# A quadrant swap by DMA alone: queues fed in coupled turns instead of a deep free-running queue

## The chip, the cores and the metric

The kernel runs on one core of one Trainium2 chip. The metric is the device time of the whole launch in microseconds (us); smaller is better. Several runs of each kernel are compared by their median.

## The reference

```python
def setup_inputs():
    return {"x": np.random.randn(8192, 8192).astype(np.float32)}

def reference(x):
    return np.fft.ifftshift(x)
```

For an even number of rows and columns this moves the four quadrants: output row r, left half, is input row (r + 4096) mod 8192, right half; and output row r, right half, is the same input row's left half. Nothing is computed. A half row is 4096 float32, 16 KB, contiguous in memory; rows are 32 KB apart. There are 16384 half rows, 268.44 MB to be read and as much to be written.

## The kernel before, in words

The data never enters the core's own memory. Every transfer is a DMA (`dma_start`) that reads half rows of `x` and writes them as half rows of `out`, both in the chip's large memory (HBM). Two of the core's instruction sequencers issue the DMAs, each on a queue of its own: `nc.sync` (SP, the queue that the profile calls q1) and `nc.scalar` (ACT, q10). Sixteen DMA engines serve both queues.

The helper `copy` issues one DMA of 256 half rows, 16 for each of the 16 engines (`per = 16`, `rows = 256`). Its access pattern has three dimensions: 16 entries one row apart, then 16 entries 16 rows apart, then the 4096 numbers of a half row. So each of the 16 entries of the outermost dimension stands for the half rows of one engine, and neighbouring engines work on neighbouring rows:

```python
dims = [[C, ENGINES], [step * C, per], [1, hc]]
```

The loop takes 1024 rows at a time, in four groups of 256. SP copies the left halves of the groups in the order 0, 1, 2, 3; ACT copies the right halves in the order 2, 3, 0, 1, so that the two queues are 512 rows apart. That makes 32 DMAs for each queue, of 4 MB each.

The order is that of the program. The framework gives the DMAs eight semaphores in turn, four for each queue, and puts a wait ahead of a DMA whose semaphore is still in use: so each queue has up to four DMAs in flight, 64 half rows for each engine, and the next is issued when the oldest has landed. At the end SP waits for all of them.

Of the kernel before, what the change touches and what calls it, by code (L numbers as in the profile page):

```python
# [1 line left out]

# [4 lines left out]


ENGINES = 16


@with_exitstack
def kernel(
    ctx: ExitStack,
    tc: tile.TileContext,
    x: bass.AP,
    out: bass.AP,
):
    nc = tc.nc
    R, C = x.shape  # L20
    hr = R // 2
    hc = C // 2
    per = 16
    rows = ENGINES * per

    def copy(queue, row, h, step):

        dims = [[C, ENGINES], [step * C, per], [1, hc]]
        queue.dma_start(
            out=bass.AP(out.tensor, out.offset + row * C + h, dims),  # L30
            in_=bass.AP(x.tensor, x.offset + (row + hr) % R * C + hc - h, dims),
        )

    for first in range(0, R, 4 * rows):
        for n in range(4):
            copy(nc.sync, first + n * rows, 0, ENGINES)
            copy(nc.scalar, first + (n + 2) % 4 * rows, hc, ENGINES)


# [1 line left out]
_INS = ['x']  # L43
_OUTS = [((8192, 8192), 'float32')]


def kernel(**inputs):
    import numpy as _np
    import concourse.bacc as _bacc
    import concourse.tile as _tile  # L50
    from concourse import mybir as _mybir
    from concourse.bass_utils import run_bass_kernel_spmd as _run

    nc = _bacc.Bacc("TRN2", target_bir_lowering=False, num_devices=1)  # L54
    arrays, args = {}, []
    for name in _INS:
        a = _np.ascontiguousarray(inputs[name])
        if a.dtype.kind in "iu":
            a = a.astype(_np.int64)
        arrays[f"in_{name}_dram"] = a  # L60
        args.append(nc.dram_tensor(f"in_{name}_dram", a.shape, _mybir.dt.from_np(a.dtype), kind="ExternalInput").ap())
    for i, (shape, dtype) in enumerate(_OUTS):
        dt = _mybir.dt.from_np(_np.dtype(dtype))
        args.append(nc.dram_tensor(f"out_{i}_dram", shape, dt, kind="ExternalOutput").ap())
    with _tile.TileContext(nc) as tc:
        kernel(tc, *args)
    r = _run(nc, [arrays], core_ids=[0])
    got = tuple(r.results[0][f"out_{i}_dram"] for i in range(len(_OUTS)))
    return got[0]
```

## Time and profile before

| | |
|---|---|
| runs | 815.96, 812.23, 815.3 us; median 815.3 |
| span of the profiled execution | 812.4 us (its own time is not given apart from the span; the span lies beside the lowest of the runs) |
| DMAs | 32 from SP, 32 from ACT, 4096 KB each |
| time of one issue, median | SP 571 ns, ACT 578 ns |
| first issue, last landing | 0.73 us, 811.5 us after the span's start |
| issue to landing | shortest 25.6, median 101.0, longest 103.4 us |
| moved | 268.44 MB read and 268.44 MB written |

How to read it: a DMA is cut into packets, here one of 16 KB for each half row and one of 4 bytes for each engine that reports its completion. The rows "DMA" and "GB/s" of a view cut its window into 40 slices and give the busy share of the 16 DMA engines and the bytes that they moved in each; a row that begins with a queue's name gives its packets, its megabytes and the time of its packets as a share of 16 engines' time. "L29" is the line that issues the DMAs. "SPq" is the sequencer of SP, whose waits are listed with their total, number and longest.

### The profile page before, as it was taken

The numbers are of one execution on the slowest core, as the hardware profiler recorded it, in microseconds if no ns is written. First come the engines' busy times: TensorE is split into PE (matmuls) and PEld (weight loads), VectorE is DVE, ScalarE is ACT, GpSimd is POOL, SyncE is SP. The second block draws the span as 40 slices with busy tenths as digits, with TensorE's granted clock in tenths as the row PEclk, the third lists the DMA queues.
The fourth block names the chain that finished last, engine by engine and source line by source line (L and its number), as shares of the span: only waits on it lengthen the run. The fifth ranks groups of instructions, "written<-read, shape, count | busy, mean of one in ns | idle before, by whom it ended". The sixth has DMA issues, their size and how long they took to land. (4 is left out here: it accounts for less than half of the span.)

```text
span 812.4 us, 109 instructions
## 1 busy us (share of the span) xinstructions
POOL 0.2 (0%) x4
## 2 busy tenths in 40 slices
POOL 0000000000000000000000000000000000000000
DMA  9999999999999999999999999999999999999998
GB/s 307 331 331 336 335 331 331 335 325 337 334 332 336 331 333 332 334 339 332 332 334 331 329 331 334 332 328 333 330 334 335 334 328 333 332 331 330 338 331 280
DMA packets 17408, 268.44 MB, mean 330 GB/s; under 512 B 1024, under 2 KB 1024, under 8 KB 1024
## 3 DMA queue, kind: packets, MB, share of 16 engines
q1 hardware_dynamic: 8704, 134.22, 49.7%
q10 hardware_dynamic: 8704, 134.22, 49.5%
HBM read 268.44 MB, written 268.44 MB: 661 GB/s over the span
## 5 line engine op out<-in xcount | busy, mean ns | idle before, releaser
L54 POOL MEMSET const-bfloat16-1.0<- 128x1 bf16 x1 | 0.1, 101 | 0.0
L54 POOL MEMSET const-uint8-127<- 128x1 uint8 x1 | 0.1, 101 | 0.0
L54 POOL MEMSET const-float32-0.0<- 128x1 f32 x1 | 0.1, 98 | 0.2 <-issue 0.2
L54 POOL MEMSET const-float32-1.0<- 128x1 f32 x1 | 0.1, 98 | 0.0
## 6 DMA issues: line engine op xcount, KB each, us to landing
out_dram<-in_x_dram SPq DMA_DIRECT2D x32, 4096.0 KB, 101.0
out_dram<-in_x_dram ACTq DMA_DIRECT2D x32, 4096.0 KB, 101.0
```

The lines of the kernel that those rows point to most:

```text
L54: nc = _bacc.Bacc("TRN2", target_bir_lowering=False, num_devices=1)
```

## The change

The transfers stay DMAs of half rows on the same two queues; their sizes, their access pattern and the moment at which they are issued change.

- The access pattern has two dimensions: 16 x per rows, one row apart, and the 4096 numbers of a half row. How the rows are divided among the 16 engines is no longer written out.
- The rows are taken in eight eighths of 1024 rows, each with its own entry (turn, rest) of `plan`. A turn gives each engine `turn` half rows on each queue (8 or 16). It is issued as two DMAs for each queue: a main part of `turn - rest` half rows per engine, and an end part of `rest`.
- Before a turn is issued, both sequencers wait until the main parts of all turns before it have landed, those of both queues. At that moment `rest` half rows per engine are left on each queue. `main0`, `main1`, `end0` and `end1` are the semaphores that count this, by 16 for each DMA.
- In the fifth eighth, `rest` is 0: its turns are issued without a wait and undivided.
- ACT works 512 rows away from SP within the same eighth, as before.
- The whole stands in a critical section, in which the framework places no waits of its own. SP waits for all semaphores at the end.

The DMAs of one queue become: eighths one to four, 16 DMAs each (8 turns; main parts of 4, 3, 2 and 1 half rows per engine, end parts of 4, 5, 6 and 7); eighth five, 8 DMAs of 8 half rows per engine; eighths six to eight, 8 DMAs each (4 turns; main parts of 12, 10 and 8, end parts of 4, 6 and 8). That is 96 for each queue, 192 in all.

```diff
-    per = 16
-    rows = ENGINES * per
-
-    def copy(queue, row, h, step):
+    def copy(queue, row, h, per, sem):
 
-        dims = [[C, ENGINES], [step * C, per], [1, hc]]
+        dims = [[C, ENGINES * per], [1, hc]]
+        dst = out.offset + row * C + h
+        src = x.offset + (row + hr) % R * C + hc - h
         queue.dma_start(
-            out=bass.AP(out.tensor, out.offset + row * C + h, dims),
-            in_=bass.AP(x.tensor, x.offset + (row + hr) % R * C + hc - h, dims),
-        )
+            out=bass.AP(out.tensor, dst, dims),
+            in_=bass.AP(x.tensor, src, dims),
+        ).then_inc(sem, ENGINES)
 
-    for first in range(0, R, 4 * rows):
-        for n in range(4):
-            copy(nc.sync, first + n * rows, 0, ENGINES)
-            copy(nc.scalar, first + (n + 2) % 4 * rows, hc, ENGINES)
+    part = 1024
+    plan = ((8, 4), (8, 5), (8, 6), (8, 7), (8, 0), (16, 4), (16, 6), (16, 8))
+
+    with tc.tile_critical(), ExitStack() as sems:
+        mains = [sems.enter_context(nc.semaphore(f"main{i}")) for i in range(2)]
+        ends = [sems.enter_context(nc.semaphore(f"end{i}")) for i in range(2)]
+        queues = (nc.sync, nc.scalar)
+        main = end = 0
+        for k, (turn, rest) in enumerate(plan):
+            rows = ENGINES * turn
+            for first in range(k * part, (k + 1) * part, rows):
+                other = k * part + (first - k * part + part // 2) % part
+                if rest:
+                    for queue in queues:
+                        for sem in mains:
+                            queue.wait_ge(sem, main)
+                for queue, row, h, m, e in zip(
+                    queues, (first, other), (0, hc), mains, ends
+                ):
+                    copy(queue, row, h, turn - rest, m)
+                    if rest:
+                        copy(queue, row + ENGINES * (turn - rest), h, rest, e)
+                main += ENGINES
+                end += ENGINES if rest else 0
+        for sem in mains:
+            nc.sync.wait_ge(sem, main)
+        for sem in ends:
+            nc.sync.wait_ge(sem, end)
```

## The prediction, made before the changed kernel ran

> **What bounds the kernel now.** I read the page first, then the DMA view in short windows at the start and the end, then the queue's own waits and the landings of the output tensor, then the packet and landing records themselves. The page:
>
> ```profile
> DMA  9999999999999999999999999999999999999998
> ...
> DMA packets 17408, 268.44 MB, mean 330 GB/s; under 512 B 1024, under 2 KB 1024, under 8 KB 1024
> ...
> q1 hardware_dynamic: 8704, 134.22, 49.7%
> q10 hardware_dynamic: 8704, 134.22, 49.5%
> ```
>
> No compute engine works. The 16 DMA engines are busy 49.7 + 49.5 = 99.2% of 812.4 us, 805.9 us. Of the 17408 packets, 1024 are the small completion writes (64 DMAs x 16 engines) and 16384 are half rows of 16 KB, 1024 for each engine. So a half row holds its engine for 805.9 / 1024 = 0.787 us, and 1% of that is 8.1 us of kernel. The packet records add two things: there are always 14 to 17 packets in flight, one for each engine, each starting within about 10 ns of the end of the one before; and a third of them take the shortest time, 0.611 us, the others up to 1.4. The kernel is therefore the packet time multiplied by 1024, plus two ends. Nothing that only changes when a packet is queued can shorten it, unless it changes how long a packet takes.
>
> Does the packet time move during the run? Stretches of the span (length, POOL busy, clock, DMA share, GB/s):
>
> ```profile
> 2.20:5.00 2.80, 0.00 (x0) 1.00 1.00 351
> 5.00:10.00 5.00, 0.00 (x0) 1.00 1.02 360
> 10.00:15.00 5.00, 0.00 (x0) 1.00 0.99 311
> ...
> 100.00:400.00 300.00, 0.00 (x0) 1.00 1.00 333
> 400.00:800.00 400.00, 0.00 (x0) 1.00 1.00 332
> ```
>
> It is fast for the first 8 us and flat afterwards. Between 2.1 and 5.0 us only q1 (SP's queue) has data, and 64 packets go by, four for each engine in 2.9 us, 0.725 each. The second and third packet of each engine average 0.62 and 0.67 us.
>
> The waits of SP's queue, and the last 12 us:
>
> ```profile
> SPq L29 <- DMA out_dram<-in_x_dram: 689.4, 28, 25.3
> SPq L65 <- DMA out_dram<-in_x_dram: 102.2, 2, 79.5
> ```
> ```profile
> 806.00:808.00 2.00, 0.00 (x0) 1.00 0.96 328
> 808.00:810.00 2.00, 0.00 (x0) 1.00 0.54 180
> 810.00:812.40 2.40, 0.00 (x0) 1.00 0.02 7
> ```
>
> The sequencers already wait on landings, 28 times, but with four DMAs of 16 half rows in flight on each queue, so each engine has some 100 us of work ahead (median to landing 101.0 us). None of those waits reaches an engine. In the landing records the 16 engines finish one DMA within 1.1 to 2.8 us of each other all through the run, so they do not drift apart; the ACT queue stays some 3.5 packets per engine behind SP's, the head start of the first 2.9 us.
>
> **The change part by part.**
>
> *Bytes and half rows.* The same 16384 half rows of 16 KB, on the same two queues, with the same left and right halves 512 rows apart. Cost 0.
>
> *More DMAs.* 64 become 192: in four eighths 8 turns x 2 queues x 2, in the fifth 8 x 2, in the last three 4 x 2 x 2. Issuing takes 0.571 us each (SP) or 0.578 (ACT); 96 for each sequencer is 55 us of 812, beside the transfers. Completion writes go from 64 to 192 per engine; one takes 9 ns in the records and the next half row starts 6 ns later, so 128 x 15 ns = **1.9 us**, on the path, since engines have no gaps. Bounds: 0 and, if every gap of the run was due to them, (808 - 805) / 64 x 128, about 5 us.
>
> *The waits at a turn.* There are 44 turns that wait, 32 of 8 half rows and 12 of 16. Before it issues, each sequencer waits until the main part of the turn before has landed from both queues; behind the wait stands only that sequencer's next issue. An engine then has `rest` half rows left on each queue, 2 x rest x 0.787 us of work: 6.3, 7.9, 9.4, 11.0 and 12.6 us for rest 4 to 8. What must fit under it: from the packet's end to its landing 0.39 us (24.34 to 24.73 in the records), from issue to first packet 2.16 - 0.73 = 1.43 us, the lead of the fastest engine, up to 2.8 us, and SP's lead over ACT, one packet here, as a main part of 64 rows should delay ACT's first packet by 64/256 of the 2.9 us seen at the start. For rest 4 this is 0.4 + 1.4 + 2.8 + 0.8 = 5.4 against 6.3 us. It fits narrowly at 4 and well from 5 on. The cover is the rest part; without it a turn would cost over 2 us. For the 16-row turns with rest 4, SP's main part is 192 rows, ACT may fall 2.2 us behind, and a fast engine could go dry for a moment. I take **0.5 us** over the 12 turns of rest 4; bounds 0 and 12 x 2 = 24 us.
>
> *One drain.* The fifth eighth has rest 0: its main semaphores count whole turns. The first turn of the sixth eighth therefore waits until everything has landed, and the engines stand idle. This costs the mean wait for the slowest engine, 2.1 us by the last stretches above (0.46 of 2.0 us, and 0.98 of 1.2 us up to the last packet at 811.2), or 1.2 us by the mean over landings; then 0.39 us to land, 0.1 for the wait, 1.43 to the first packet, and 0.2 as first packets take 1.05 us. Sum 3.3 to 4.2; I take **4.0 us**. It is the only stall written into the program.
>
> *Ends.* A critical section adds a handshake of the two sequencers ahead of the first issue and another after the last wait. Such handshakes are 0.4 to 0.7 us in the waits of before, and may overlap with what is there: **0.6 us** together, bounds 0 and 1.5.
>
> *Which rows an engine works on.* Before, the outermost dimension has 16 entries one row apart, so the engines work on neighbouring rows, 32 KB apart. Now one dimension of 16 x per rows is split over the engines. If each gets a run of rows, they stand per x 32 KB apart, 32 to 384 KB, different in each eighth; if they get every sixteenth, nothing changes. The trace has no addresses and only the one spacing. From below, the cost is bounded by the start's pace, 1024 x (0.725 - 0.787) = -63 us; from above by a slow stretch of the trace, 311 against 333 GB/s, +57 us. Both come from stretches under 10 us, and every long stretch gives 332 or 333, so I take the long rows: 0. The Trainium skill speaks against the change here: "DMA: Bandwidth & Descriptors", section "Latency and other measured facts", has copies between HBM tensors at 207 GB/s with a row pitch of 512 KiB, 164 at 2 MiB and 214 at full rate. By that ratio, as an estimate, the whole run at a 512 KiB spacing would be 812.4 x 214/207 = 840 us. No run here shows it yet.
>
> Sum: 1.9 + 0.5 + 4.0 + 0.6 + 0 = 7.0 us. On the profile's span 812.4 that is 819.4. The runs shown have a median of 815.3, 2.9 above the span, so I forecast **822**.
>
> **The rivals.**
>
> *Aligned engines copy faster.* Short turns could keep engines and queues in the ordered state of the start, in which a half row takes 0.725 us or less. If one packet in three keeps that, 341 x 0.062 = 21 us are won: 815.3 + 7 - 21 = 801. For it: the second and third packets at 0.62 to 0.67. Against: the pace is gone by 10 us although the engines are then still within 1.6 us of each other, and 1.4 or 2.5 us of spread go with the same 333 and 332 GB/s. A turn that finds its queues filled lines up nothing. It decides the sign once one packet in nine keeps the pace (7.0 / 0.062 = 113 packets). Chance 0.24.
>
> *The new spacing collides.* If engines further apart meet more often in memory, the share of packets at 0.611 us falls. It is 0.32 now, so the others average (0.787 - 0.32 x 0.611) / 0.68 = 0.870; at a share of 0.25 the mean is 0.805, +18 us: 840. For it: two thirds of the packets are already stretched. Against: nothing in the trace shows that spacing matters. The rule of the skill above would be this case, and its steps are larger pitches than any here. Chance 0.17.
>
> *Rest 4 is too short.* Each of the 12 turns of rest 4 runs dry by 1 us: 815.3 + 7 + 12 = 834. Chance 0.07.
>
> *Nothing is felt.* The drain lies in ACT's tail, the small writes are free: 815. Chance 0.12.
>
> **How the numbers follow.** Forecast 0.40. About 0.5% is what a measurement of this kernel can tell from no change, here 811.2 to 819.4. Faster: the first rival without its weakest outcomes, 0.22, and 0.02 of the forecast. Same: the last rival 0.12, 0.06 of the forecast, 0.02 of the first. Slower: 0.32 + 0.17 + 0.07. The range 800 to 840 holds the forecast, the drain and starved cases, and half of each of the two rivals about packet time (0.40 + 0.12 + 0.07 + 0.12 + 0.09 = 0.80). The forecast's own range is 817 to 828, from the bounds of its small terms.
>
> **What would show it.** By eighths of the span: a DMA share of 1.00 everywhere but one dip of about 4 us near 510 us; 3072 small packets; GB/s of 331 to 333 in every eighth. The layout rival shows as GB/s that differ between eighths with a full DMA share, lowest where engines are furthest apart (eighths five to eight). Starvation shows as a share under 1.00 in the first and sixth eighth alone. The first rival shows as GB/s above 340 in the first four eighths. I am wrong if the packet time changes by over 1%, since every other term is small.

## The result, and the profile after

The changed kernel takes 815.93 us (median of 18 runs, 814.11 to 818.22), the kernel before 812.39 us (18 runs beside it, 809.84 to 816.83). The ratio is 1.0037, with a 95% interval of 1.002 to 1.0053: slower by 3.0 us by the ratio and 3.5 by the medians, within the 0.5% that the prediction called no change, and half of the 0.8% that it forecast.

The page of the changed kernel (busy tenths and GB/s in 40 slices of 20 us, packets, queues):

```profile
DMA  8999999999999999999999998999999999999998
GB/s 295 334 332 334 335 334 334 329 339 336 330 333 338 334 337 334 330 337 332 329 330 340 333 336 281 336 330 331 335 333 334 330 330 333 336 333 336 327 333 283
DMA packets 19458, 268.46 MB, mean 330 GB/s; under 512 B 3072, under 2 KB 3072, under 8 KB 3072
...
q10 hardware_dynamic: 9728, 134.22, 49.9%
q1 hardware_dynamic: 9728, 134.22, 48.8%
```

Between the two ends all slices look like those of before but one, the 25th, at 281 GB/s. Stretches around it:

```profile
502.00:504.00 2.00, 0.00 (x0) 1.00 0.96 328
504.00:506.00 2.00, 0.00 (x0) 1.00 0.45 172
506.00:508.00 2.00, 0.00 (x0) 1.00 0.00 0
508.00:510.00 2.00, 0.00 (x0) 1.00 0.84 295
510.00:512.00 2.00, 0.00 (x0) 1.00 1.14 418
```

That is the drain. In the records the last half row ends at 506.5 us, the turn is released at 507.1 and the first new packet starts 1.3 us later, 1.9 us after that last end. The last 16 half rows had ended 1.1 us before the very last on average, and the first 16 new ones start 0.2 us after the first on average. Adding up, moment by moment, what is missing from 16 half rows in flight, the fifth eighth has 3.8 us of idle time and the other eighths without an end 0.6 to 1.3, about as much as in the kernel before (0.5 to 0.8): the drain holds the engines for 2.8 to 3.2 us, by which of the two is taken off. The short excess at 418 GB/s behind it resembles the fast start that the prediction saw at the beginning of the run; it lasts 2 us.

Stretches within the eighths, first to fourth and sixth to eighth:

```profile
2.40:100.00 97.60, 0.00 (x0) 1.00 1.00 334
102.00:200.00 98.00, 0.00 (x0) 1.00 1.00 334
203.00:300.00 97.00, 0.00 (x0) 1.00 1.00 334
304.00:400.00 96.00, 0.00 (x0) 1.00 1.00 334
...
510.00:600.00 90.00, 0.00 (x0) 1.00 0.99 333
610.00:700.00 90.00, 0.00 (x0) 1.00 1.00 333
710.00:806.00 96.00, 0.00 (x0) 1.00 1.00 333
```

Turns of 8 or 16, with 4 to 8 left, all move 333 or 334 GB/s with engines fully busy: neither starvation nor an effect of the spacing. SP's queue waits:

```profile
SPq L55 <- DMA out_dram<-in_x_dram: 710.1, 43, 115.7
```

There are 43 waits in place of 28, and apart from the one at the drain no stretch shows one that reaches an engine.

What remains is the packet time. The mean in the records is 0.7829 us, against 0.7865 before, 3.7 us over 1024 packets, and that gain was in nobody's sum. The experiments are about the drain, this gain, the completion writes, and the bounds that the prediction left wide.

Two sorts of numbers must be kept apart. The time of a run is 1.8 us over its span. By that, the profiled execution of before took 814.2 us and lies 1.8 us above the median of 18, while the one of the changed kernel (815.5) lies at its median. So profiles show 1.4 us between the kernels, and medians 3.5.

Of the experiments, the first four ran beside a kernel before of 813.5 us; the next four with an interval beside one of 822.6 and the last four beside one of 822.0, each group on a chip of its own. The kernel before is about 1.1% slower in the later two groups, and so is the mean packet: 0.781 to 0.785 us in the profiles of the first group, 0.791 to 0.796 in those of the others. Times are therefore compared within such a group, and ratios across them. The second profile of before and the two sweeps by eighths are single executions on a fourth chip.

### The profile page after: what moved, and what is told of

It reads as the page before. It is cut to its first block, busy times and chain, and to the rows that moved or that the text cites. A ratio compares the mean times of both kernels' runs of the same rounds, so it can differ in the third digit from the quotient of the medians.

```text
span 813.8 us, 332 instructions
## 1 busy us (share of the span) xinstructions
POOL 0.2 (0%) x4
```

## The experiments

**Layout alone, and layout put back.** The kernel before with the new pattern, and the changed kernel with the old one:

```diff
-        dims = [[C, ENGINES], [step * C, per], [1, hc]]
+        dims = [[C, ENGINES * per], [1, hc]]
```


> The kernel before with nothing but the two-dimensional access pattern (256 rows one row apart) in the 64 free-running DMAs. Profile of the changed kernel: a half row takes 0.7829 us against 0.7865, which is 1024 x 0.0036 = 3.7 us won and hides half of the costs. Theory L (the division of rows among engines makes the packets shorter): mean packet 0.783, ratio to before 0.9955. Theory Q (the two queues in step, a lead of 0.25 packets per engine in place of 2.5) and theory D (few half rows queued, turns): 0.7865, ratio 1.000. Theory N (the two profiles differ by chance, runs of one kernel spread by 0.8%): 1.000, mean packet anywhere in 0.782 to 0.790.


```diff
-        dims = [[C, ENGINES * per], [1, hc]]
+        dims = [[C, ENGINES], [ENGINES * C, per], [1, hc]]
```


> The changed kernel with the access pattern of before (16 entries one row apart, then steps of 16 rows) and all its turns and waits. Theory L: packets go back to 0.7865, 3.7 us slower than the changed kernel, ratio to before 1.008. Theories Q, D, N: same as the changed kernel, ratio 1.0037, within 1.002 to 1.0053.

Layout alone: 813.09 us, ratio 1.0002 (0.9985 to 1.0018), mean packet 0.7847. Layout put back: 814.93 us, 1.002 (1.0002 to 1.0038), mean packet 0.7833, and the dip is there again, near 507 us, with 4.5 us of idle time in that eighth. Theory L falls: the new pattern does not make the kernel faster, and the old one does not make the changed kernel slower.

**The drain moved to the end of the plan, and turns further ahead.**

```diff
-    plan = ((8, 4), (8, 5), (8, 6), (8, 7), (8, 0), (16, 4), (16, 6), (16, 8))
+    plan = ((8, 4), (8, 5), (8, 6), (8, 7), (16, 4), (16, 6), (16, 8), (8, 0))
```


> The changed kernel with the entry without waits moved from the fifth to the last place of the plan, so that no turn waits for everything to land. All theories: the dip near 506 us is gone, and with it the 3.2 us that the engines stood idle in that eighth beyond the others: ratio to before 1.0037 - 0.0039 = 0.9998. If the drain is paid back elsewhere (engines start again in order and run faster for a while) the gain is under 2 us: ratio over 1.0013.

For the second kernel, each turn takes one of four pairs of main semaphores and waits for its last use, four turns ago:

```diff
...
+                mains = lanes[lane]
-                if rest:
+                if rest and used[lane]:
                     for queue in queues:
                         for sem in mains:
-                            queue.wait_ge(sem, main)
+                            queue.wait_ge(sem, used[lane])
...
```


> As the kernel with the drain moved to the end, but a turn waits for the main parts of the fourth turn before it, not of the last, so that three more turns (24 or 48 half rows per engine and queue) stay queued; the number of DMAs and completion writes is the same. Theory D (few half rows queued make packets shorter): packets at 0.7865, 3.7 us slower than the kernel with the drain at the end, ratio about 1.004. Theories L, Q and N: the same as that kernel, ratio about 1.000, as the lead of the queues is set at the start by the small first DMAs in both.

Drain at the end: 812.18 us, 0.9986 (0.9967 to 1.0006), 2.75 us under the kernel with the old pattern, which has the drain and ran beside it. Where the dip was:

```profile
502.00:504.00 2.00, 0.00 (x0) 1.00 0.92 311
504.00:506.00 2.00, 0.00 (x0) 1.00 1.07 393
506.00:508.00 2.00, 0.00 (x0) 1.00 0.99 344
508.00:510.00 2.00, 0.00 (x0) 1.00 1.02 328
```

The engines are busy throughout. The deep turns gave 814.16 us, 1.0005 (0.9985 to 1.0025). That is 2 us more than the short turns, in the direction of theory D, which had 3.7; but the lead between the queues was 3.0 packets here and 0.9 there, so that theory Q would say the same, and the intervals overlap. (The lead is counted here as the half rows that one queue has started more than the other, per engine, as a mean over the run. By this count the kernel before has 3.3 and the changed kernel 0.9; the expectations have smaller figures for both, which this count does not give.) Its profile even has the shortest mean packet of the four, 0.7808, in a run of 809.8 us.

**The lead alone, own waits, larger turns, twice the DMAs.**

The kernel before, with the first DMA of each queue in four:

```diff
...
+            if first == 0 and n == 0:
+                for i in range(4):
+                    copy(nc.sync, i * 64, 0, ENGINES, 4)
+                    copy(nc.scalar, 2 * rows + i * 64, hc, ENGINES, 4)
+                continue
```


> The kernel before, free-running, with the first DMA of each queue cut into four of 4 half rows per engine, and nothing else. It was made to take the lead of one queue over the other away (2.5 packets per engine in the kernel before, 0.25 to 0.6 in the kernels with short turns, 2.5 in the kernel with deep turns). The traces so far show the second queue's first packet 2.8 to 2.9 us after the first queue's, with first DMAs of 64 and of 256 rows alike, so the cut may leave the lead where it is; the trace tells. Theory Q (queues in step make packets shorter): if the lead falls under 1, ratio 0.9975 (2 us won); if it stays, 1.000. Theory D (few half rows queued): 1.000 in either case.

The kernel with the drain at the end, each sequencer waiting for its own queue:

```diff
-                    for queue in queues:
-                        for sem in mains:
-                            queue.wait_ge(sem, main)
+                    for queue, sem in zip(queues, mains):
+                        queue.wait_ge(sem, main)
```


> The kernel with the drain at the end (812.2 us, 0.9986 of before), but each sequencer waits for its own queue's main part alone, so that the queues are kept short and not in step: one queue may lead by 2 to 3 packets all along. Theory Q: the 2 us against the kernel with deep turns are lost, ratio 1.001. Theory D: kept, ratio 0.9986. Theory N (the 2 us between the short and the deep turns were chance): anything from 0.998 to 1.001, and the kernels of this call scatter likewise.

One plan throughout, with 128 DMAs:

```diff
-    plan = ((8, 4), (8, 5), (8, 6), (8, 7), (8, 0), (16, 4), (16, 6), (16, 8))
+    plan = ((16, 6),) * 8
```


> Turns of 16 half rows, 6 left, in all eight eighths: 128 DMAs in place of 192, no drain, no eighth without waits. Theory D and Q: the packets as short as in the kernel with the drain at the end, and 64 fewer completion writes per engine x 15 ns = 1.0 us less: 811.2 us, ratio 0.9975, the fastest version. Theory N: 1.000 less nothing, 0.999 to 1.001.

In the kernel with the drain at the end, every DMA of over one half row per engine in two, on the same semaphore (`one` issues a single DMA, as `copy` did):

```diff
+        if per > 1:
+            one(queue, row, h, per // 2, sem)
+            one(queue, row + ENGINES * (per // 2), h, per - per // 2, sem)
+            return 2 * ENGINES
...
```


> The kernel with the drain at the end, every DMA of more than one half row per engine cut into two: 368 DMAs in place of 192, 176 more completion writes for each engine. If one costs 15 ns, as the prediction took it, 2.6 us more: 814.8 us, ratio 1.0018. If the writes are free, 812.2 and 0.9986. If a DMA has a larger cost of its own on the engines (0.1 us or more each), over 830 us.

| | us | ratio (interval) | lead, packets | queued |
|---|---|---|---|---|
| lead, first DMAs cut | 823.30 | 0.9995 (0.9974 to 1.0016) | 3.3 | deep |
| own waits | 823.32 | 1.0004 (0.9987 to 1.0021) | 3.1 | short |
| turns of 16, 6 left | 821.98 | 0.9993 (0.9976 to 1.001) | 1.5 | short |
| twice the DMAs | 822.62 | 0.9998 (0.9982 to 1.0014) | 0.7 | short |

The cut did not take the lead away: the second queue's first packet is again 3.0 us behind. So it says nothing on theory Q. The others do not part Q from D either; every interval holds 1.000. No version is measurably faster than the kernel before, and the 2 us of the earlier pair have not come back.

**The kernel before, profiled once more.** No edit.

> The kernel before once more, for a second profile. If the mean packet of 0.7865 us in its first profile was typical, it comes back within 0.0005. If the packet time itself is what varies from run to run (runs spread by 7 us, 0.9%), it follows the span: 1 us of span for each 1.0 ns of mean packet.

Span 809.0 us, mean packet 0.7826. Between two executions of the same kernel the packet time moved by 3.9 ns and the span by 3.4 us: as much as the gain that was to be explained. The packet time therefore moves with the execution or the chip, which these two profiles do not part, and a single profile does not give it to better than half a per cent. This fits theory N; that nothing else shortened the packets is not shown.

**Four drains and none.** The same 128 DMAs in two orders, in place of the plan of the changed kernel:

```diff
+    plan = ((8, 0), (16, 8)) * 4
```


> The turns of the changed kernel with the plan (8, 0), (16, 8) four times over: four turns wait until everything has landed, in place of one; 128 DMAs. If a drain costs what the engines stood idle in the changed kernel (3.2 us): 4 x 3.2 = 12.7 us more than the same turns without drains, a ratio between the two of 1.016. If most of it is given back by faster packets behind it: under 1.008. If the cause of the changed kernel's 0.37% is not the drain: no difference beyond 0.2%.


```diff
+    plan = ((16, 8),) * 4 + ((8, 0),) * 4
```


> The same turns in another order, (16, 8) four times and then (8, 0) four times: the same 128 DMAs of the same sizes, and no turn that waits for everything. Ratio to before 0.998 to 1.001, as the other kernels without a drain; no dip in the DMA share.

With four drains 835.5 us (5 runs), 1.0166 (1.014 to 1.0192); without, 822.87 us (12 runs), 1.0016 (0.9999 to 1.0034). The difference is 12.6 us, 3.2 us for each drain; by the two intervals it is uncertain by some 2.6 us. The two profiles differ by 12.6 us as well: 11.0 us of that is idle time of the engines, 2.8 us for each drain, and 1.6 us is packet time (0.7956 against 0.7940 us). The page of the kernel with four drains:

```profile
DMA  8999999999999999999999998999999999899998
GB/s 294 334 328 325 326 295 326 320 332 336 318 329 328 323 314 305 326 328 324 329 330 324 330 329 294 321 327 329 321 332 328 332 328 333 280 334 325 329 326 284
```

Dips of the GB/s stand at the 6th, the 15th and 16th, the 25th and the 35th slice, one behind each eighth without waits; a slice is 20.8 us here, so that 294 of 328 is 2.2 us of work missing, and the second dip is split over two slices.

**Completion writes on one chip.** The kernel with the drain at the end, and its twin with twice the DMAs, side by side:

> The kernel with the drain at the end of the plan once more (192 DMAs), for its twin with twice the DMAs on the same chip: ratio to before 0.9986 if the first result holds, 0.998 to 1.001 if all kernels without a drain are alike.

> The kernel with every DMA cut in two once more (368 DMAs): 176 more completion writes per engine than the kernel with the drain at the end. At 15 ns each 2.6 us more than that kernel (0.32%); at 3 ns, as the first comparison with 128 DMAs suggests, 0.5 us (0.06%).

821.97 us, 0.9999 (0.9981 to 1.0017), against 822.67 us, 1.0011 (0.9994 to 1.0028). The 176 more writes of each engine cost 0.7 us, 4 ns each, and that with an uncertainty larger than itself; 2.6 us would stand at its edge. By this pair the 128 writes that the change adds cost about 0.5 us, where the prediction had 1.9, but the pair alone does not exclude 1.9. The kernel before bounds them better: against it, the kernel with twice the DMAs has 304 more writes per engine, which at 15 ns are 4.6 us or 0.55%. It came out at 0.9998 and 1.0011, with intervals that end at 1.0014 and 1.0028. So 15 ns each does not fit, unless the turns win something back elsewhere; the higher of the two ends allows about 8 ns each, 1.0 us for 128 writes.

**How little may be left.**

```diff
-    plan = ((8, 4), (8, 5), (8, 6), (8, 7), (8, 0), (16, 4), (16, 6), (16, 8))
+    plan = ((8, 7), (8, 5), (8, 4), (8, 3), (8, 2), (8, 1), (16, 2), (16, 1))
```


> The changed kernel with the plan 8 turns each of rest 7, 5, 4, 3, 2, 1 (turns of 8) and 4 turns each of rest 2, 1 (turns of 16). It looks for the rest at which engines run dry. By the prediction's sum (0.4 to land, 1.4 from issue to packet, up to 2.8 of spread, against 1.57 us for each half row left on both queues): idle time under 0.3 us per turn for rest 4 and more; at rest 3 (4.7 us of cover) the fastest engines run dry, 0.1 to 0.5 us per turn; at rest 2 (3.1) 0.5 to 1.5; at rest 1 (1.6) 1.5 to 2.5. Against it: no idle time at rest 3 and 2, if the spread of the engines counts for less than the prediction took.

Its eighths in order, ends left out:

```profile
5.00:100.00 95.00, 0.00 (x0) 1.00 1.00 334
105.00:200.00 95.00, 0.00 (x0) 1.00 1.00 333
206.00:300.00 94.00, 0.00 (x0) 1.00 1.00 334
307.00:405.00 98.00, 0.00 (x0) 1.00 0.98 328
410.00:514.00 104.00, 0.00 (x0) 1.00 0.92 311
519.00:625.00 106.00, 0.00 (x0) 1.00 0.89 302
632.00:730.00 98.00, 0.00 (x0) 1.00 0.96 324
737.00:838.00 101.00, 0.00 (x0) 1.00 0.94 315
```

With 7, 5 and 4 left the engines stay busy. At 3 the eighth has 3.6 us of idle time, against 0.6 to 0.8 in those three: 0.35 us per turn. At 2 it is 1.2 us per turn, at 1 it is 1.6, and with turns of 16 the same (1.1 and 1.6). So the cover that a turn needs lies between 4.7 us (3 left) and 6.3 us (4 left).

**How far apart engines may work.** The kernel before, with the rows of neighbouring engines 1, 16, 32 and 64 rows apart, twice over; over 1, the 16 half rows of an engine in one DMA follow one another:

```diff
-        dims = [[C, ENGINES], [step * C, per], [1, hc]]
+        dims = [[space * C, ENGINES], [step * C, per], [1, hc]]
...
```


> The kernel before, free-running, with the engines' rows 1, 16, 32, 64, 1, 16, 32, 64 rows apart in the eight eighths (32 KB, 512 KB, 1 MB, 2 MB); within an engine the rows follow one another where the spacing is over 1. The layout rival of the prediction: GB/s lower at 512 KB by 3% (a packet of 0.81 us), and by over 20% at 2 MB. No effect of spacing: 331 to 334 GB/s in each eighth.

Its eighths (32 KB, 512 KB, 1 MB, 2 MB, and again):

```profile
10.00:100.00 90.00, 0.00 (x0) 1.00 1.00 333
110.00:200.00 90.00, 0.00 (x0) 1.00 0.99 333
212.00:325.00 113.00, 0.00 (x0) 1.00 1.00 269
337.00:465.00 128.00, 0.00 (x0) 1.00 0.99 235
480.00:570.00 90.00, 0.00 (x0) 1.00 1.00 333
580.00:670.00 90.00, 0.00 (x0) 1.00 1.00 334
682.00:795.00 113.00, 0.00 (x0) 1.00 1.00 265
808.00:940.00 132.00, 0.00 (x0) 1.00 1.00 238
```

Up to 512 KB the spacing is free. At 1 MB the mean packet is 0.98 us, at 2 MB 1.10, and the DMA share stays at 0.99 to 1.00: busy is not the same as fast. In the 2 MB eighths the two queues work 32 rows apart, in the others 512 rows, so the loss at 2 MB is not shown to be due to the engines' spacing alone; the step from 512 KB to 1 MB has no such second difference.

## Why the prediction was right or wrong

*What bounds the kernel* held: packets one behind the other, 1024 for each engine, in every kernel here.

*The drain* held in mechanism and nearly in size: 4.0 us forecast, 2.8 to 3.2 measured in idle time and 3.2 by the runs with four. Its mis-sized part is the wait for the slowest engine. The prediction took 2.1 us from the end of the run; ahead of the drain it was 1.1 us. The way from the last end to the first new packet was forecast at 0.39 + 0.1 + 1.43 = 1.9 us and took 1.9. The drain is the one term that the runs show clearly: the two kernels with the change's single drain are at 1.0037 and 1.002, the kernels in turns without one between 0.9986 and 1.0016, and the one with four at 1.0166.

*The sum* is the step that failed: its terms were mis-sized, 7.0 us in all against 3.5 by the medians. Beside the drain there were 1.9 for completion writes, 0.5 for rest 4 and 0.6 for the ends. The ends held: the first packet is 0.2 us later, and the span goes on 0.4 us longer after the last landing. Rest 4 shows no idle time that stands out (0.6 us in its eighth where the rest was varied). The largest miss is the writes: about 0.5, at most about 1.0 by the bound above. What failed for them is the count of small gaps: 9 ns of a record and 6 ns to the next packet were summed as if the 16 engines lost them. (The upper bound beside that term, about 5 us, is 6 by its own figures.) Engines that share a memory may get a little of such a gap back; that is argued, not shown. In place of 7.0 stands 3.2 + 0.5 + 0.6 = 4.3 us; the medians differ by 3.5 and the interval reaches from 1.6 to 4.3. The kernels without a drain come out at 1.000 within 0.2%, so the smaller terms are below what these runs can tell.

*The level* was off by nearly as much. The forecast put its sum on a median of three runs, 815.3, and left unused that the span alone was 812.4; with 18 runs the median is 812.39. That is 2.9 of the 6.1 us between 822 and 815.93.

*A wrong step that did not count:* ACT's first packet was to lag by 64/256 of 2.9 us. In the changed kernel ACT went first, and SP followed 2.8 us later, with first DMAs of 64 rows. The prediction scaled the lag from a first DMA of 256 rows, but it is no longer at 256 rows than at 64. Below 64 rows it does follow the size: 1.7 to 1.8 us with first DMAs of 32 rows (the kernel with twice the DMAs) and 0.7 us with 16 rows (the kernel that varies how little is left). In short turns that wait for both queues the lead became small all the same, 0.6 to 0.8 packets in most eighths of the changed kernel and 1.9 in the one behind the drain.

*The rivals.* Aligned engines: the state exists, but has to be bought with a standstill. In the eighth with 1 left the packets are 0.771 us against 0.783, a gain of 1.5 us over 128 packets for 13 us of idle time. A turn that finds its queues filled has no such gain: 334 GB/s. Spacing: the mechanism is real, and begins between 512 KB and 1 MB, beyond the 384 KB that the change can reach; the 840 us was not borne out. The rule of the Trainium skill that the prediction weighed ("DMA: Bandwidth & Descriptors", section "Latency and other measured facts") comes, as an estimate from its 207, 164 and 214 GB/s, to 97% of the full rate at a row pitch of 512 KiB and 77% at 2 MiB. Here, with the spacing between engines as the pitch, it is 100% at 512 KB (333 and 334 of 333 GB/s) and 71% at 2 MB (235 and 238): the trace agrees that large spacings cost, and not that 512 KB does. Rest 4 too short: off by one half row; the sum of 5.4 us lies between the 4.7 that starve and the 6.3 that do not. Nothing is felt: wrong on the drain, nearer on the writes. That its 815 lies closest to the measured 815.93 is luck: its base was 2.9 us too high, and the drain that it left out costs 3.2.

*Still open:* whether short, coupled turns shorten packets by the 1 to 2 us that lie between the 4.3 of the terms and the lower medians. The pairs that were to tell it agree with zero. Whether an engine's rows in the new pattern follow one another or are 16 apart cannot be read from the time either, since both spacings are free.

## What to carry to other kernels

Where engines never stop and every queue is filled, no order or depth of issue that was tried here made the kernel measurably faster. Find the one place where a wait covers everything that is queued, and price it as the spread of the engines there, the landing, and the way from issue to first packet (3.2 us here). A wait in mid-stream was free here as long as more was queued than that same chain takes: the limit lies between 4.7 and 6.3 us of work for each engine. And set a forecast of under 1% on the run that the trace belongs to, not on a median of three; a packet time from one profile is no better than the spread of the runs.

## What the runs showed of the hardware that was not expected

- The second of the two queues starts 2.8 to 3.0 us behind the first, whichever is first, when the first DMA has 64 to 256 rows; in that time the first queue moves four packets per engine. With a first DMA of 32 rows the lag is 1.7 to 1.8 us and the first queue moves two packets per engine (32 in all), with 16 rows 0.7 us and one (14 in all before the other queue's first). Four half rows per engine seem to go ahead of the other queue, or the first DMA where that is smaller.
- A spacing of 1 MB between the 16 engines' rows costs 20% of the bandwidth (269 and 265 GB/s against 333), and 512 KB nothing. At 2 MB the loss was 29%, with the two queues closer together as well.
- A sequencer that issues without waits is held by the DMA instruction itself. The eighth DMA of 128 rows in the eighth without waits took 2.5 us to issue on SP where the others took 0.6, and in the kernel with four drains three on SP took 11.1 to 11.7 us. In the kernel with the same DMAs and no drain, whose last four eighths have no waits, most DMAs of these eighths were held for some 11 us and three on SP for 33; it was not measurably slower for it (1.0016, 0.9999 to 1.0034).
